# Attention outputs from four 64x64 tiles, a PSUM bank shared with the scores, and outputs placed behind the scores

## The chip, the cores and the metric

The kernel runs on one core of a Trainium2 chip. The metric is device time in microseconds (us). Five engines work side by side: TensorE (PE, matrix products), VectorE (DVE), ScalarE (ACT), GpSimd (POOL) and SyncE (SP, which issues the DMAs). Each takes its own instructions strictly in order. Matrix products land in PSUM, which has eight banks of 128 partitions x 512 float32; a bank is free for the next product when everybody has read the last one out of it.

## The reference

A trunk of two residual layers for 1024 tokens of width 1024: first a retention and RWKV-7 mixer, then sliding-window attention, each followed by a gated feed-forward block, and a last RMSNorm. The change lies in the attention of the second layer:

```python
q, k, v = jnp.split(z, [SWA_WIDTH, SWA_WIDTH + SWA_KV_HEADS * HEAD_DIM], axis=-1)
...
kb, vb = with_prev(k), with_prev(v)
s = jnp.einsum('bnqhgd,bnkhd->bnhgqk', q, kb).astype(jnp.float32) * HEAD_DIM ** -0.5
band = (rel >= 0) & (rel < W)
...
m = jnp.maximum(jnp.max(s, axis=-1, keepdims=True), sink)
e = jnp.exp(s - m)
p = e / (jnp.sum(e, axis=-1, keepdims=True) + jnp.exp(sink - m))
o = jnp.einsum('bnhgqk,bnkhd->bnqhgd', p.astype(vb.dtype), vb)
```

There are 16 query heads of 64, in four groups that share one key and value head each. The queries go in blocks of 128; a query sees the 128 keys that end at its own place, so of a block's 256 keys (its own block and the one before) exactly 128 are used by each query.

## The kernel before, in words

Large products run in a split form: each float32 operand is cut into a high part, rounded to TensorE's single-pass float type, and the rest, and three products (high x high, high x rest, rest x high) are summed in PSUM. A weight of 128 x 1024 comes by DMA (`wload`, L402), ScalarE casts the high part (L432), VectorE or GpSimd subtracts the rest (L433). TensorE is filled with such products (lines 1306, 1308, 1309 in `prod` and 447, 449, 450 in `gemm`), 24 of them for one weight tile and half of the 1024 tokens; they go to the three PSUM buffers `ps_f`. This text calls them filling products.

Attention stands inside such filling. The 16 work items, called pairs here, are (half of the tokens, key head, two query blocks). For a pair j the plan `ATTN_PLAN` has four steps:

- **S**, `scores`: 24 programmed products (20 where the first block has no predecessor), each on a 64x64 tile of TensorE (L1726), to the banks `ps_r`, `ps_c` and twice `ps_m`. Only the band is computed: for each query the score against key x of its own block and of the block before share one place, because only one of the two is inside the window. ScalarE copies one part out (L1737, L1739), VectorE lays the other over it under a mask (L1740), takes the row maximum (L1758) and joins it with the sink (L1759), ScalarE takes eight exponentials, one per head and block (L1763), VectorE adds, inverts and multiplies (L1766 to L1768), and transposes 32x32 blocks (L1773); a DMA writes the result to DRAM (`pd`).
- **D**, `fetch`: four DMAs read it back with the keys on the partitions (`pc`, L1780).
- **M**, `sides`: VectorE multiplies `pc` by a triangle, which gives the part of the own block `pT` (L1787), and VectorE and GpSimd subtract it, one half each, which leaves in `pc` the part of the block before (L1792).
- **O**, `out`: for each of two blocks and two heads of a row, the own block's values times `pT` and the earlier block's values times `pc`, 8 products of 128 keys x 64 (L1805) into one bank `ps_y`. Half of each product's entries are zeros. ScalarE rounds the high part out of PSUM (L1811) and VectorE subtracts for the rest (L1812).

`kv` computes keys and values of a half: the values are transposed with four matmuls per 128 columns into `vt` (L1678), which ScalarE copies (L1679). The letters q, k, r, w, f, p in the plan are steps of the filling: query and key projections, the attention's output projection, the forming of the next block's inputs (`form0`, behind an RMS sum, L479) and the first feed-forward products (`early`, with a copy L1472 out of PSUM between their two halves).

The order on the engines is set by a scheduler, except where `behind` pins one instruction after another, and on TensorE in this stage, where `ATTN_ORDER` fixes the order of all products: each entry is the number of a PSUM tile, in the order in which the tiles first appear, and how many of its products come next.

Of the kernel before, what the change touches and what calls it, by code (L numbers as in the profile page):

```python
# [32 lines left out]
for _n, _w in (  # L33
# [19 lines left out]
def make_consts():  # L53
# [45 lines left out]
    put("amask", np.concatenate([np.where(x[:, None] == x[None, :], own, 0.0), own.T], axis=1))  # L99
# [38 lines left out]
S8 O5 M6 D7 rr S9 O6 M7 D8 S10 O7 M8 D9 wwwwk S11 kwwww rr f rr S12 rr O8 M9 D10 p S13 O9 M10 D11 pp S14 O10 M11 D12 p  # L138
# [116 lines left out]
class Kern:  # L255
    def __init__(self, ctx, tc, A, out):
# [990 lines left out]
    def normed(self, out, hf, k, g, r):  # L1247
        self.nc.vector.scalar_tensor_tensor(
            out=out, in0=self.kt(self.h[hf])(k), scalar=self.col(g, k), in1=r, op0=ALU.mult, op1=ALU.mult
        )  # L1250

    def form0(self, g, r, n8, sp):

        self.X = {nm: [self.hl(n8, k + o) for k in range(4)] for nm, o in (("11", 0), ("21", 4))}
        for nm, o in (("11", 0), ("21", 4)):
            for k in range(4):
                f = self.u0(sp)
                self.normed(f, 0, k + o, g, r)
                self.nc.sync.dma_start(self.bd[k + o], f)
                self.split(f, *self.X[nm][k], False)  # L1260
# [357 lines left out]
    def attn_open(self, ap):  # L1618
        nc = self.nc
        m = self.const(ap, "amask").rearrange("p (m o t) -> p m o t", m=2, o=1)  # L1620
        self.own = m[:, 0].rearrange("p o (x t) -> p o x t", x=2).to_broadcast([P, 2, 2, 64]).bitcast(mybir.dt.uint32)
        self.key = m[:, 1].rearrange("p o (q t) -> p q o t", q=4).to_broadcast([P, 4, 8, 32])
# [9 lines left out]
        self.nu0 = 0  # L1632
        self.akv, self.aq, self.ch = {}, ([], []), {}

    def proj(self, nr, ti, out, **kw):
# [7 lines left out]
        self.nc.vector.tensor_tensor(out=out, in0=ps, in1=nr[1], op=ALU.mult)  # L1643
        self.nc.scalar.activation(out, out, AF.Identity, **kw)

    def kv(self, hf, nr, ap):
# [4 lines left out]
        vt = self.t(ap, [P, 5, 256], "vt", 2)  # L1651
# [40 lines left out]
    def attn(self, ap, outs, fill, plan):  # L1692
# [52 lines left out]
        def scores(j):  # L1745
# [20 lines left out]
            V.tensor_tensor(out=den, in0=den, in1=es, op=ALU.add)  # L1766
# [10 lines left out]
        def fetch(j):  # L1777
            pc = pcs[j] = self.t(ap, [P, 4, 8, 32], "pc", 2)
            for k in range(4):
                nc.sync.dma_start(  # L1780
                    pc[32 * k : 32 * k + 32].rearrange("p q h t -> p q (h t)"), ds[j][:, :, k].rearrange("q t x -> t q x")
                )

        def sides(j):
            pc = pcs[j]
            pT = pTs[j] = self.t(ap, [P, 4, 8, 32], "pT", 2)
            x = V.tensor_tensor(out=pT, in0=pc, in1=self.key, op=ALU.mult)  # L1787
            if j + 2 in sinks:
                self.behind(x, sinks[j + 2])
            for i, e in enumerate((V, G)):  # L1790
                h = slice(4 * i, 4 * i + 4)
                e.tensor_tensor(out=pc[:, :, h], in0=pc[:, :, h], in1=pT[:, :, h], op=ALU.subtract)  # L1792

        def out(j):
# [16 lines left out]
            S.copy(hi, po)  # L1811
# [283 lines left out]
```

## Time and profile before

| | us |
|---|---|
| median of 3 runs | 2266.25 |
| range of the runs | 2265.46 to 2266.54 |
| the profiled execution | 2264.58 |
| its span in the trace | 2261.8 |
| TensorE busy | 2221.5 |
| VectorE busy | 1683.9 |
| ScalarE busy | 1011.3 |
| GpSimd busy | 1009.9 |

The span runs from the first to the last instruction; the profiled execution has 2.8 us around it. The pairs' scores start at 1363.7 us and their last output ends at 1628.1 us; the rest of the program stays as it is.

### The profile page before, as it was taken

Reading aid. Unit: us, or ns where it says so; the run is one execution under the profiler, and the core shown is the slowest. Engines: PE = TensorE matmul, PEld = TensorE weight load, DVE = VectorE, ACT = ScalarE, POOL = GpSimd, SP = SyncE. Lnnn points to the kernel's source line nnn. Section 1 sums busy time; section 2 is a strip of 40 time slices with the busy share of each in tenths; the row PEclk is TensorE's granted clock in tenths of the full one; section 3 lists DMA queues with packets and bytes.
Section 4 is the critical chain, followed back from the end, with each engine's and each line's share of the span. In section 5 each row is a group of like instructions: output and inputs, shape, how many; then the busy total and the mean of one; then the engine's idle time right before and its main releaser. Section 6 shows DMA issues by size and latency. Waiting matters only on the chain.

```text
span 2261.8 us, 36143 instructions
## 1 busy us (share of the span) xinstructions
PE 2221.5 (98%) x13296; PEld 1784.8 (79%) x13296; DVE 1683.9 (74%) x2476; ACT 1011.3 (45%) x1914; POOL 1009.9 (45%) x784
## 2 busy tenths in 40 slices
PE   8999999999999999999999999998999999999998
PEld 6777777777878888888888887776788888888886
DVE  7877965875667358888887877987457788888876
ACT  5454544424455333333433466656444333333335
POOL 3123221202341067777787610104203677777676
PEclk9999999999999999999999999999999999999999
DMA  8565654443446545665676334444546565658663
GB/s 282 188 219 203 201 158 135 141 118 117 148 181 195 205 160 209 214 210 206 242 259 246 131 113 133 162 140 155 176 150 229 176 213 211 208 202 292 225 216 117
DMA packets 181856, 423.22 MB, mean 187 GB/s; under 512 B 44464, under 2 KB 55344, under 8 KB 181680
## 3 DMA queue, kind: packets, MB, share of 16 engines
q1 hardware_dynamic: 178272, 414.37, 53.4%
q10 hardware_dynamic: 2832, 4.45, 0.5%
q8 instruction: 105, 1.72, 0.3%
q0 software_dynamic: 576, 2.10, 0.2%
q14 instruction: 71, 0.58, 0.1%
HBM read 283.87 MB, written 131.60 MB: 184 GB/s over the span
## 4 chain that ended last, share of the span: by engine, by line
PE 77%; DVE 10%; ACT 4%; issue 3%; DMA 3%; POOL 2%; SPq 1%; DVEq 0%; POOLq 0%; ACTq 0%
PE ps_f L291 11%; PE ps_m L1306 8%; PE ps_m L1309 7%; PE ps_m L1308 7%; PE ps_m L291 6%; PE ps_f L1306 5%; PE ps_f L1308 5%; PE ps_f L1309 5%; PE ps_r L1306 2%; PE ps_c L1309 2%; PE ps_c L1306 2%; PE ps_r L1309 2%; PE ps_r L1308 2%; PE ps_c L1308 2%; PE ps_f L449 2%
## 5 line engine op out<-in xcount | busy, mean ns | idle before, releaser
L291 PE MATMUL ps_f<-n,w 128*128 128x512 f32 x1440 | 358.6, 402 | 8.6 <-ACT w L432 5.7
L291 PEld LDWEIGHTS ps_f<-n,w 128*128 128x128 f32 x1440 | 266.5, 189 | 83.4 <-issue 12.6
L433 POOL TENSOR_TENSOR w<-wr,w 128x512 fp32r<-128x512 f32 x63 | 88.3, 1411 | 294.8 <-ACT w L432 293.4
L432 ACT CAST w<-wr 128x512 fp32r<-128x512 f32 x231 | 140.7, 617 | 153.8 <-PE ps_f L450 48.7
L1306 PE MATMUL ps_f<-n,w 128*128 128x512 f32 x415 | 164.6, 397 | 0.5 <-ACT q L1472 0.5
L1309 PE MATMUL ps_f<-n,w 128*128 128x512 f32 x415 | 162.5, 392 | 0.0
L433 DVE TENSOR_TENSOR w<-wr,w 128x512 fp32r<-128x512 f32 x168 | 118.2, 708 | 59.2 <-ACT w L432 58.7
L1308 PE MATMUL ps_f<-n,w 128*128 128x512 f32 x415 | 162.2, 391 | 0.0
L433 POOL TENSOR_TENSOR w<-wq,w 128x512 fp32r<-128x512 f32 x91 | 130.8, 1449 | 31.0 <-ACT w L432 31.0
L1306 PE MATMUL ps_m<-n,w 128*128 128x512 f32 x333 | 130.4, 392 | 0.0
L1308 PE MATMUL ps_m<-n,w 128*128 128x512 f32 x333 | 129.6, 389 | 0.0
L1309 PE MATMUL ps_m<-n,w 128*128 128x512 f32 x333 | 129.5, 389 | 0.0
L1316 DVE TENSOR_TENSOR nq<-ps_m,u 128x512 f32<-128x512 f32 x88 | 58.9, 684 | 93.9 <-PE ps_m L1309 93.8
L464 POOL TENSOR_TENSOR n<-nq,n 128x512 fp32r<-128x512 f32 x60 | 100.1, 1679 | 7.6 <-ACT n L462 7.6
L1501 POOL TENSOR_TENSOR w<-wd,w 128x512 fp32r<-128x512 f32 (+1 forms) x62 | 87.1, 1414 | 33.1 <-ACT w L1500 32.7
L1306 PEld LDWEIGHTS ps_f<-n,w 128*128 128x128 f32 x415 | 77.9, 188 | 21.9 <-issue 3.8
L1306 PE MATMUL ps_m<-cb,w 128*128 128x512 f32 x236 | 91.9, 389 | 0.3 <-DVE nq L1316 0.3
L1308 PE MATMUL ps_m<-cb,w 128*128 128x512 f32 x236 | 91.8, 389 | 0.0
L1309 PE MATMUL ps_m<-cb,w 128*128 128x512 f32 x236 | 91.8, 389 | 0.0
L1309 PEld LDWEIGHTS ps_f<-n,w 128*128 128x128 f32 x415 | 77.9, 188 | 17.1 <-issue 0.7
L1501 POOL TENSOR_TENSOR w<-ws,w 128x512 fp32r<-128x512 f32 (+1 forms) x48 | 71.6, 1497 | 44.4 <-ACT w L1500 40.7
L1308 PEld LDWEIGHTS ps_f<-n,w 128*128 128x128 f32 x415 | 77.9, 188 | 16.6 <-issue 1.0
(539 smaller groups left out, 6347.9 us busy)
## 6 DMA issues: line engine op xcount, KB each, us to landing
hc<-n SPq DMA_DIRECT2D x84, 512.0 KB, 3.2
wsp<-w SPq DMA_DIRECT2D x54, 512.0 KB, 3.3
w<-wsp SPq DMA_DIRECT2D x54, 512.0 KB, 3.4
n<-hc SPq DMA_DIRECT2D x54, 512.0 KB, 6.2
wq<-in_w_gate SPq DMA_DIRECT2D x44, 512.0 KB, 4.5
u<-u SPq DMA_DIRECT2D x76, 256.0 KB, 3.1
ha<-hc SPq DMA_DIRECT2D x34, 512.0 KB, 5.2
hid<-n SPq DMA_DIRECT2D x66, 256.0 KB, 2.0
```

The lines of the kernel that those rows point to most:

```text
L291: i = self.nc.tensor.matmul(out, lhsT, rhs, **kw)
L432: nc.scalar.copy(hi[:, :n], raw[:, c])
L433: self.lo.tensor_tensor(out=lo[:, :n], in0=raw[:, c], in1=hi.bitcast(F32)[:, :n], op=ALU.subtract)
L449: y = nc.tensor.matmul(ps, hi, rl, start=False, stop=False)
L464: e.tensor_tensor(out=lo, in0=src, in1=hi.bitcast(F32), op=ALU.subtract)
L1306: i = mm(ps, hi, xh, start=first and k == 0, stop=False, skip_group_check=True)
L1308: mm(ps, hi, xl, start=False, stop=False, skip_group_check=True)
L1309: mm(ps, lo, xh, start=False, stop=last and k == len(w) - 1, skip_group_check=True)
L1316: self.last_add = V.tensor_tensor(out=o, in0=x, in1=y, op=ALU.add)
L1501: nc.gpsimd.tensor_tensor(out=lo, in0=v, in1=hi.bitcast(F32), op=ALU.subtract)
```

## The change

`out` becomes 20 products of 64 keys x 64 (16 in the first pair of a head), each on one 64x64 tile of TensorE, and leaves out the squares that hold only zeros. Rows 0 to 63 of the tiles work on the first block of the pair and rows 64 to 127 on the second; the first goes to `ps_y`, the second to `ps_c`, the bank that the scores use as well. For that the keys have to lie by halves: the values of the current half and of the other are laid down for both blocks in `vt` (2 x 4 x 256 for each partition where it was 5 x 256), which takes 20 transposing products in the first half of the tokens and 16 in the second where it was 8 and 8, and the value projection is stored with its columns rearranged (`halves`). The probabilities are fetched with the matching rearrangement, in pieces of 128 where it was 256 floats. `sides` now has a triangle only in two of the four squares: `pT` and the subtraction are 512 elements long where the first was 1024, and both run on VectorE. High part and rest of the outputs are taken out in two pieces, one from each bank. In the order, O stands 12 filling products (once 18) behind S in ten of the pairs where it stood right behind it, and new pins (`behind`) set where the output's copies, the subtractions, some copies of the feed-forward's first half (`u0copies`) and one product of `form0` (`formed`) stand.

```diff
-S8 O5 M6 D7 rr S9 O6 M7 D8 S10 O7 M8 D9 wwwwk S11 kwwww rr f rr S12 rr O8 M9 D10 p S13 O9 M10 D11 pp S14 O10 M11 D12 p
+S8 O5 M6 D7 rr S9 O6 M7 D8 O7 wwrr S10 M8 D9 wkw S11 wkwww rr f S12 rr O8 M9 D10 p S13 O9 M10 D11 pp S14 O10 M11 D12 p
...
-17:12 22:24 23,24:8 25,26:12 27:24 28:12 29,30:12 31,32:12 33:6 28:12 34:24 35,36:8 37,38:12 39:8 40:24 41:12 42,43:12
+22,23:12 19:12 24:24 25,26:8 27,28:12 29:24 30:12 31,32:12 33,34:12 30:12 35:2 36:2 35:2 36:2 35:2 36:6 37:24 38,39:8
...
     def kv(self, hf, nr, ap):
-        vt = self.t(ap, [P, 5, 256], "vt", 2)
+        vt = self.t(ap, [P, 2, 4, 256], "vt", 2)
...
         for i, vc in enumerate(vcs):
-            pt = self.pst("m", [P, 4, P])
-            for b in range(4):
-                nc.tensor.transpose(pt[:, b, :], vc[:, P * b : P * b + P], self.cst["ident"])
-            nc.scalar.copy(vt[:, 1:5, P * i : P * i + P], pt)
+            ds = slice(P * i, P * i + P)
+            for prev in range(2):
+                pt = self.pst("m", [P, 2, 2, P])
+                for m in range(2):
+                    for r in range(2):
+                        c = 256 * r + 64 * (2 * m - prev)
+                        if m >= prev:
+                            nc.tensor.transpose(pt[:, m, r], vc[:, c : c + P], ident)
+                            continue
+                        nc.tensor.matmul(pt[64:, m, r], vc[:, c + 64 : c + P], ident, start=True, stop=True, skip_group_check=True)
+                        if not hf:
+                            nc.tensor.transpose(pt[:64, m, r], vc[:, c + 256 : c + 320], ident)
...
         def sides(j):
             pc = pcs[j]
-            pT = pTs[j] = self.t(ap, [P, 4, 8, 32], "pT", 2)
-            x = V.tensor_tensor(out=pT, in0=pc, in1=self.key, op=ALU.mult)
+            pT = pTs[j] = self.t(ap, [P, 2, 2, 4, 32], "pT", 2)
+            d = pc.rearrange("p r (x q) h t -> p (r x) (q h t)", x=2)[:, 0:4:3]
+            o = pT.rearrange("p x q h t -> p x (q h t)")
+            x = V.tensor_tensor(out=o, in0=d, in1=self.key, op=ALU.mult)
             if j + 2 in sinks:
                 self.behind(x, sinks[j + 2])
-            for i, e in enumerate((V, G)):
-                h = slice(4 * i, 4 * i + 4)
-                e.tensor_tensor(out=pc[:, :, h], in0=pc[:, :, h], in1=pT[:, :, h], op=ALU.subtract)
+            subs[j] = x, V.tensor_tensor(out=d, in0=d, in1=o, op=ALU.subtract)
 
         def out(j):
...
-            po = self.pst("y", [P, 2, 2, P])
-            pv = [x[j].rearrange("p q (b i e) t -> p b e i q t", b=2, e=2) for x in (pcs, pTs)]
-            for i in range(2):
-                kbs = (1,) if hf == 0 and b0 + i == 0 else (1, 0)
-                for kb in kbs:
+            po = [self.pst(x, [P, 2, P]) for x in "yc"]
+            c, o = (x[j].rearrange("p r q (i e) t -> p r e i q t", e=2) for x in (pcs, pTs))
+            lo, hi, every = slice(0, 2), slice(2, 4), slice(0, 4)
+            parts = [
+                (0, lambda e: c[:, 0, e, :, hi], hi), (0, lambda e: o[:, 0, e], lo), (1, lambda e: o[:, 1, e], hi),
+                (2, lambda e: c[:, 0, e, :, lo], lo), (3, lambda e: c[:, 1, e], every),
+            ]
+            for y, (kind, src, x) in enumerate(parts):
+                for i in range(2):
+                    first = hf == 0 and b0 + i == 0
+                    if first and kind > 1:
+                        continue
+                    rs = slice(64 * i, 64 * i + 64)
                     for e in range(2):
                         mm(
-                            po[64 * e : 64 * e + 64, i], vt[:, b0 + i + kb, 64 * g : 64 * g + 64], pv[kb][:, i, e],
-                            start=kb == 1, stop=kb == kbs[-1], skip_group_check=True,
+                            po[i][64 * e : 64 * e + 64, :, 32 * x.start : 32 * x.stop],
+                            vt[rs, b0 // 2, kind, 64 * g : 64 * g + 64], src(e)[rs],
+                            start=y == 0, stop=y > 3 or first and y > 0, skip_group_check=True,
                         )
...
-            S.copy(hi, po)
-            V.tensor_tensor(out=lo, in0=po, in1=hi.bitcast(F32), op=ALU.subtract)
+            for i in range(2):
+                his[j] = S.copy(hi[:, i], po[i])
+                los[j] = V.tensor_tensor(out=lo[:, i], in0=po[i], in1=hi[:, i].bitcast(F32), op=ALU.subtract)
...
+        at = -1
+        for w in plan.split():
+            j = int(w[1:]) if w[0] in do else -1
+            if w[0] == "S":
+                at, seen = j, set()
+            elif j >= 0 and at >= 0 and w[0] not in seen:
+                seen.add(w[0])
+                if w[0] == "O":
+                    self.behind(exps[at], his[j])
+                if w[0] == "M":
+                    self.behind(dens[at], subs[j][1])
+            if w[0] == "M" and j and j < 13:
+                self.behind(subs[j][0], los[j - 1])
+        for j, i in ((12, 0), (14, 3), (15, 4)):
+            self.behind(exps[j], self.u0copies[i])
+        self.behind(self.formed[5], los[8])
```

On TensorE, around the output of the second pair, the end of the scores and the output stand like this before (`n` and `w` are inputs of filling products):

```order
L1726 MATMUL ps_m_13255<-ks_1913_12469,q_1969_12808 64x64
L1726 MATMUL ps_m_13254<-kc_1908_12433,q_1969_12808 64x64
L1805 MATMUL ps_y_13292<-pT_13171,vt_12393 64x256 x2
L1805 MATMUL ps_y_13292<-pc_13034,vt_12393 64x256 x2
L1805 MATMUL ps_y_13292<-pT_13171,vt_12393 64x256 x2
L1805 MATMUL ps_y_13292<-pc_13034,vt_12393 64x256 x2
L1306 MATMUL ps_f_13322<-n_1943_12697,w_13316 128x512
```

and with the change the output itself is

```order
L1317 MATMUL ps_f_13362<-n_1946_12714,w_13356 128x512
L1845 MATMUL ps_y_13319<-pc_13049,vt_12393 64x2x64 x2
L1845 MATMUL ps_c_13320<-pc_13049,vt_12393 64x2x64 x2
L1845 MATMUL ps_y_13319<-pT_13199,vt_12393 64x2x64 x2
L1845 MATMUL ps_c_13320<-pT_13199,vt_12393 64x2x64 x2
L1845 MATMUL ps_y_13319<-pT_13199,vt_12393 64x2x64 x2
L1845 MATMUL ps_c_13320<-pT_13199,vt_12393 64x2x64 x2
L1845 MATMUL ps_y_13319<-pc_13049,vt_12393 64x2x64 x2
L1845 MATMUL ps_c_13320<-pc_13049,vt_12393 64x2x64 x2
L1845 MATMUL ps_y_13319<-pc_13049,vt_12393 64x256 x2
L1845 MATMUL ps_c_13320<-pc_13049,vt_12393 64x256 x2
L1314 MATMUL ps_f_13362<-n_1947_12715,wx_13359 128x512
```

The output moved from right behind its scores to 12 filling products behind them, and half of it writes `ps_c`, whose last content is the first part of those scores.

On ScalarE at the same place, before: the copies of the scores, the output's high part, the eight exponentials (`s`, with the sink's `st` among them).

```order
L1739 COPY s_13238<-ps_m_13254 128x2x128
L1644 ACTIVATE kc_2028_13198<-kc_2028_13198,pv_67 128x512
L1811 CAST n_2016_13154<-ps_y_13292 128x2x2x128
L1763 ACTIVATE s_13238,st_13272<-s_13238,st_13272 128x128 x3
L1761 ACTIVATE st_13272<-st_13272 128x8
L1763 ACTIVATE s_13238,st_13272<-s_13238,st_13272 128x128 x5
```

With the change:

```order
L1768 COPY s_13265<-ps_m_13281 128x2x128
L440 CAST w_13638<-wr_13636 128x512
L1792 ACTIVATE s_13265,st_13299<-s_13265,st_13299 128x128 x3
L1790 ACTIVATE st_13299<-st_13299 128x8
L1792 ACTIVATE s_13265,st_13299<-s_13265,st_13299 128x128 x4
L1853 CAST n_2018_13169<-ps_y_13319 128x2x128
L1853 CAST n_2018_13169<-ps_c_13320 128x2x128
L1792 ACTIVATE s_13265,st_13299<-s_13265,st_13299 128x128
```

The output's copies moved from ahead of the exponentials to ahead of the last one.

On VectorE at the same place, before: the masks of the scores, the maximum, the output's rest, and behind the joining with the sink the work of step M.

```order
L1740 COPY_PREDICATED s_13238<-c_amask_12331,ps_m_13254 128x2x128
L1758 TENSOR_REDUCE st_13272<-s_13238 128x8
L1812 TENSOR_TENSOR n_2020_13158<-ps_y_13292,n_2016_13154 128x2x2x128
L1759 TENSOR_TENSOR st_13272<-st_13272,nsink_12335 128x8
L1760 TENSOR_TENSOR st_13272<-st_13272,sink_12333 128x8
L1787 TENSOR_TENSOR pT_13303<-pc_13175,c_amask_12331 128x1024
L1792 TENSOR_TENSOR pc_13175<-pc_13175,pT_13303 128x4x128
```

With the change:

```order
L1787 TENSOR_REDUCE st_13299<-s_13265 128x8
L441 TENSOR_TENSOR w_13638<-wr_13636,w_13638 128x512
L1788 TENSOR_TENSOR st_13299<-st_13299,nsink_12335 128x8
L1789 TENSOR_TENSOR st_13299<-st_13299,sink_12333 128x8
L1854 TENSOR_TENSOR n_2022_13173<-ps_y_13319,n_2018_13169 128x2x128
L1854 TENSOR_TENSOR n_2022_13173<-ps_c_13320,n_2018_13169 128x2x128
L1821 TENSOR_TENSOR pT_13345<-pc_13202,c_amask_12331 128x512
L1656 TENSOR_TENSOR nq_13353<-ps_f_13362,rs_12737 128x4x2x64
L1824 TENSOR_TENSOR pc_13202<-pc_13202,pT_13345 128x2x256
L1796 TENSOR_TENSOR st_13299<-st_13299 128x8
```

The output's rest moved from ahead of the joining (L1759, now L1788) to behind it, and step M stands behind the rest.

## Rows read from the trace of the kernel before

**Rows 1.** Windows: stretch, length, PE, PEld, DVE, ACT, POOL busy (x), clock, DMA share, GB/s.

```profile
1393.20:1461.30 68.10, 67.41 (x561) 51.12 (x560) 64.82 (x108) 43.72 (x158) 9.45 (x8) 1.00 0.51 168
1461.30:1522.60 61.30, 57.94 (x392) 46.24 (x392) 52.42 (x86) 35.48 (x113) 6.52 (x5) 1.00 0.42 142
...
1550.00:1628.10 78.10, 72.91 (x431) 53.80 (x431) 44.01 (x62) 40.46 (x106) 31.17 (x20) 0.93 0.53 170
1628.10:1700.00 71.90, 71.90 (x314) 58.73 (x313) 40.54 (x61) 33.74 (x54) 5.17 (x4) 1.00 0.42 146
```

**Rows 2.** Timeline of TensorE, start and length in us; scores L1726, outputs L1805.

```profile
1404.84 0.27 PE L1726 MATMUL ps_c<-ks,q 64*64 64x64 f32 x1
...
1406.11 0.65 PE L1805 MATMUL ps_y<-pT,vt 128*64 128x256 f32 x4
...
1408.53 0.50 PE L1306 MATMUL ps_f<-n,w 128*128 128x512 f32 x1
...
1461.34 0.37 PE L1726 MATMUL ps_c<-ks,q 64*64 64x192 f32 x1
```

**Rows 3.** The same timeline, the second half of the tokens; L479 is the RMS sum.

```profile
1522.59 1.02 PE L479 MATMUL ps_f<-nq,c_ones 128*128 128x512 f32 x2
...
1582.72 0.65 PE L1805 MATMUL ps_y<-pT,vt 128*64 128x256 f32 x4
...
1584.60 0.50 PE L1306 MATMUL ps_f<-n,wx 128*128 128x512 f32 x1
...
1628.10 0.50 PE L1306 MATMUL ps_f<-n,wx 128*128 128x512 f32 x1
```

**Rows 4.** Timeline of VectorE, one round whole and the ends of six rounds.

```profile
1400.36 0.42 DVE L1740 COPY_PREDICATED s<-c_amask,ps_c 128x256 f32<-128x256 uint32 x1
...
1423.69 0.41 DVE L1740 COPY_PREDICATED s<-c_amask,ps_c 128x256 f32<-128x256 uint32 x1
...
1426.27 0.68 DVE L1812 TENSOR_TENSOR n<-ps_y,n 128x512 fp32r<-128x512 f32 x1
1426.87 0.16 DVE L1759 TENSOR_TENSOR st<-st,nsink 128x8 f32<-128x8 f32 x1
...
1429.01 1.45 DVE L1792 TENSOR_TENSOR pc<-pc,pT 128x512 f32<-128x512 f32 x1
1430.44 0.17 DVE L1766 TENSOR_TENSOR st<-st 128x8 f32<-128x8 f32 x1
...
1435.56 0.44 DVE L1740 COPY_PREDICATED s<-c_amask,ps_c 128x256 f32<-128x256 uint32 x1
...
1470.12 0.43 DVE L1740 COPY_PREDICATED s<-c_amask,ps_c 128x256 f32<-128x256 uint32 x1
```

**Rows 5.** Timeline of ScalarE, the first and the last exponential of that round.

```profile
1427.12 0.40 ACT L1763 ACTIVATE s<-s,st 128x128 f32<-128x128 f32 x1 [4.43 <-DVE st L1759]
...
1429.93 0.39 ACT L1763 ACTIVATE s<-s,st 128x128 f32<-128x128 f32 x1
```

**Rows 6.** Groups by line and shape, 1360 to 1630 us: busy us, mean ns, idle before.

```profile
L1812 DVE TENSOR_TENSOR n<-ps_y,n 128x512 fp32r<-128x512 f32 x16 | 10.9, 681 | 3.2 <-ACT n L1811 3.2
L1740 DVE COPY_PREDICATED s<-c_amask,ps_c 128x256 f32<-128x256 uint32 x16 | 6.9, 432 | 2.4 <-ACT s L1737 2.4
...
L1739 ACT COPY s<-ps_m 128x256 f32<-128x256 f32 x32 | 10.3, 375 | 0.1
L1811 ACT CAST n<-ps_y 128x512 fp32r<-128x512 f32 x16 | 9.5, 592 | 11.5 <-PE ps_y L1805 11.5
...
L1792 POOL TENSOR_TENSOR pc<-pc,pT 128x512 f32<-128x512 f32 x16 | 24.3, 1521 | 136.1 <-DVE pT L1787 56.2 <-DVE st L1766 26.3 <-DMA pc<-pd 26.0
```

**Rows 7.** Waits of TensorE, 1340 to 1680 us: total us, times, longest.

```profile
PE ps_f L1306 <- ACT q L1472: 5.2, 2, 4.6
PE ps_y L1805 <- DVE n L1812: 3.2, 1, 3.2
```

**Rows 8.** The group of the value transposes, 1340 to 1640 us.

```profile
L1678 PE MATMUL ps_m<-c_ident,nq 128*128 128x128 f32 x16 | 2.5, 276 | 1.6 <-DVE s L1740 1.6
```

More of the change, by code (lines that the diff above doesn't have):

```diff
@@ L98, in make_consts @@
     x = np.arange(P) // 64
-    put("amask", np.concatenate([np.where(x[:, None] == x[None, :], own, 0.0), own.T], axis=1))
+    put("amask", np.concatenate([np.where(x[:, None] == x[None, :], own, 0.0), np.repeat(np.tile(own[:64, :64].T, (2, 1)).reshape(P, 2, 1, 32), 4, axis=2).reshape(P, 256)], axis=1))
     put("eps", np.tile(np.array([[RMS_EPS, RET_EPS, RWKV_EPS, math.log(0.5)]], np.float32), (P, 1)))
@@ L278, in __init__ @@
         self.u0s = None
+        self.u0copies, self.formed = [], []
         self.u0d = self.dram("u0", [NP, 2, P, HT])
@@ L1247, in normed @@
     def normed(self, out, hf, k, g, r):
-        self.nc.vector.scalar_tensor_tensor(
+        return self.nc.vector.scalar_tensor_tensor(
             out=out, in0=self.kt(self.h[hf])(k), scalar=self.col(g, k), in1=r, op0=ALU.mult, op1=ALU.mult
@@ L1257, in form0 @@
                 f = self.u0(sp)
-                self.normed(f, 0, k + o, g, r)
+                self.formed.append(self.normed(f, 0, k + o, g, r))
                 self.nc.sync.dma_start(self.bd[k + o], f)
@@ L1471, in early @@
         self.prod(ps, w[0](), self.X["11"], True, False)
-        self.nc.scalar.copy(u0, ps)
+        self.u0copies.append(self.nc.scalar.copy(u0, ps))
         yield
@@ L1619, in attn_open @@
         nc = self.nc
-        m = self.const(ap, "amask").rearrange("p (m o t) -> p m o t", m=2, o=1)
-        self.own = m[:, 0].rearrange("p o (x t) -> p o x t", x=2).to_broadcast([P, 2, 2, 64]).bitcast(mybir.dt.uint32)
-        self.key = m[:, 1].rearrange("p o (q t) -> p q o t", q=4).to_broadcast([P, 4, 8, 32])
+        m = self.const(ap, "amask").rearrange("p (o t) -> p o t", o=1)
+        self.own = m[:, :, :P].rearrange("p o (x t) -> p o x t", x=2).to_broadcast([P, 2, 2, 64]).bitcast(mybir.dt.uint32)
+        self.key = m[:, :, P:].to_broadcast([P, 2, 256])
         self.sink = self.t(ap, [P, 16], "sink")
@@ L1632, in attn_open, with proj @@
         self.nu0 = 0
+        self.u0copies, self.formed = [], []
         self.akv, self.aq, self.ch = {}, ([], []), {}
-    def proj(self, nr, ti, out, **kw):
+    def proj(self, nr, ti, out, halves=False, **kw):
         w = self.wload(self.A["w_qkv"][ti])
@@ L1642, in proj @@
                 yield
-        self.nc.vector.tensor_tensor(out=out, in0=ps, in1=nr[1], op=ALU.mult)
+        o, x, y = out, ps, nr[1]
+        if halves:
+            o = out.rearrange("p (r b t) -> p b r t", r=2, b=4)
+            x, y = (v.rearrange("p (b r t) -> p b r t", b=4, r=2) for v in (x, y))
+        self.nc.vector.tensor_tensor(out=o, in0=x, in1=y, op=ALU.mult)
         self.nc.scalar.activation(out, out, AF.Identity, **kw)
@@ L1671, in kv @@
             vc = self.t(self.pp, [P, HT], "nq", 4)
-            yield from self.proj(nr, 10 + i, vc, bias=self.col("bqkv", 10 + i))
+            yield from self.proj(nr, 10 + i, vc, True, bias=self.col("bqkv", 10 + i))
             vcs.append(vc)
             yield
+        every = slice(0, P), slice(0, 2)
+        ident = self.cst["ident"]
         for i, vc in enumerate(vcs):
-            pt = self.pst("m", [P, 4, P])
-            for b in range(4):
-                nc.tensor.transpose(pt[:, b, :], vc[:, P * b : P * b + P], self.cst["ident"])
-            nc.scalar.copy(vt[:, 1:5, P * i : P * i + P], pt)
+            ds = slice(P * i, P * i + P)
[10 more added lines that the diff above has]
+                            nc.tensor.transpose(pt[:64, m, r], vc[:, c + 256 : c + 320], ident)
+                for rs, m in ((slice(64, P), slice(0, 2)), (slice(0, 64), slice(1, 2))) if prev * hf else (every,):
+                    nc.scalar.copy(vt[rs, m, 2 * prev : 2 * prev + 2, ds], pt[rs, m])
+            if hf and i:
+                G.tensor_copy(vt[:64, 0, 2:4, :], pvt[:64, 0, 2:4, :])
             yield
@@ L1700, in attn @@
         ds, pcs, pTs, n8, sinks = {}, {}, {}, {}, {}
+        exps, dens, his, los, subs = {}, {}, {}, {}, {}
         def block(hf, g, b, tags, s):
@@ L1765, in scores @@
                     self.behind(y, x)
-            V.tensor_tensor(out=den, in0=den, in1=es, op=ALU.add)
+                    exps[j] = y
+            dens[j] = V.tensor_tensor(out=den, in0=den, in1=es, op=ALU.add)
             V.reciprocal(out=den, in_=den)
@@ L1777, in fetch @@
         def fetch(j):
-            pc = pcs[j] = self.t(ap, [P, 4, 8, 32], "pc", 2)
+            pc = pcs[j] = self.t(ap, [P, 2, 4, 4, 32], "pc", 2)
             for k in range(4):
+                b, k2 = k // 2, k % 2
                 nc.sync.dma_start(
-                    pc[32 * k : 32 * k + 32].rearrange("p q h t -> p q (h t)"), ds[j][:, :, k].rearrange("q t x -> t q x")
+                    pc[32 * k : 32 * k + 32].rearrange("p r q h t -> p r q (h t)"),
+                    ds[j][:, :, k2::2, P * b : P * b + P].rearrange("q t r x -> t r q x"),
                 )
```

4 lines of the change are left out of this document (1 added, 3 removed), and 21 rows, old and new, of the table ATTN_ORDER.

## The prediction

> **What bounds the kernel now.** I read the windows first, then TensorE's timeline, VectorE's timeline, the groups and TensorE's waits. In the stretch of the first half's outputs (1393 to 1461 us) TensorE is busy 67.4 of 68.1 us, and VectorE 64.8 of 68.1 [rows 1]: two engines near their limit. Without attention a filling product takes 71.9 / 314 = 0.229 us [rows 1]. The reader is to see in TensorE's timeline that an output stands where its scores end, and that 16 recorded products take 1408.53 - 1406.11 = 2.42 us there [rows 2] where an undisturbed one takes 1584.60 - 1582.72 = 1.88 [rows 3]; the 0.5 is a wait for step M. VectorE goes in rounds, one for each pair, from the mask on `ps_c` to the next one: 1423.69 to 1435.56 is 11.87 us, and the six rounds from 1400.36 to 1470.12 take 69.76, 11.63 each [rows 4]. TensorE stands ahead of VectorE: the scores of pair 9 begin at 1461.34 [rows 2], their mask at 1470.12 [rows 4], 8.8 us later. That lead is what lets TensorE stay busy.
>
> In the second half the loss is in single waits: 5.2 us of filling products for ScalarE's copy L1472 and 3.2 us of an output for VectorE's rest L1812 [rows 7], and the clock, granted 0.93 on average from 1550 to 1628 us [rows 1], which is (1 - 0.93) x 78.1 = 5.5 us at most, part of it lying in the waits. From the RMS sum at 1522.59 to the end of the last output at 1628.10 pass 105.5 us [rows 3].
>
> **The change part by part**, against the profiled execution's 2264.58 us (the median of the runs is 1.67 higher, so that much is added at the end).
>
> *Shorter outputs.* An output streams, on each of the four tiles, four pieces of 128 columns and one of 256, 768 in all; before, 1024 on each of two. No row shows a 64x64 output, but a block of scores has the same tiles and, whole, the same 768 columns: 40 recorded products of the smaller kind take 1406.11 - 1404.84 = 1.27 [rows 2], and 48 on that scale 1.5. So 1.88 becomes 1.5, 12 times: -4.6 us of TensorE's time; the four pairs without a predecessor had 12 records and gain nothing. Bounds: 1.27, and 1.88 if the tiles only overlapped in pairs.
>
> *Value transposes.* 20 more, at 2.5 / 16 = 0.16 us busy each [rows 8], less the tail that each bunch counts twice, 0.13: +2.6, between +2 and +4 (eight of them are true products, twice as long). Twelve lie in front of the first scores, where TensorE never waits: +1.5.
>
> *Step M.* GpSimd loses 24.3 us of subtractions [rows 6], VectorE's multiplication goes from 1024 elements to 512 (some 0.6 less, by the 512-long step that follows) and its subtraction falls from 1.45 [rows 4] to about the 0.6 that a 512-long step takes there (1426.27 to 1426.87 [rows 4]). With the rest in two pieces (+0.1) a round has 1.3 us less VectorE work. The 0.5 us waits of outputs for step M go.
>
> *Evacuation in two pieces.* ScalarE: 2 x 375 for 592 ns, VectorE: 2 x 432 for 681 ns by the half-sized copies and masks [rows 6], so +0.16 and +0.18 us for each pair, +2.5 and +2.9 us over the 16. I take it as hidden behind TensorE, except where a round is bound by VectorE, where the steps overlap and it is the +0.1 above; uncovered it would be +5.4. The Trainium skill ("TensorEngine Tiling (Array Packing)", Performance Considerations, PSUM Bottleneck) says that tiling speeds up TensorE but not the emptying of PSUM, which may become the bound. If that is all that counts here, the 4.6 us are gone and the sum would be 4.6 higher; by the rows above, the copies are only 5 us over 16 pairs on two engines.
>
> *The moved output and its copies.* This is the large term, and it is a loss. Before, VectorE joins maximum and sink at 1426.87 (L1759), the exponentials start at 1427.12, the eighth starts at 1429.93 [rows 5], and the sum L1766 at 1430.44 [rows 4]: 3.57 us, filled by the multiplication, a projection and the subtraction. With the change, ScalarE's order is seven exponentials, the two copies of the output, the last exponential; and VectorE's is maximum, sink, the output's rest, and only then step M. So the rest waits 0.25 + 2.8 (seven of them and the sink's) + 0.4 (a copy) = 3.5 us behind L1759, or 4.1 in every second round, where a projection's bias stands between. Ahead of it in that time stand 0.4 or 1.4 us of VectorE's work; 3.1 and 2.7 us are idle, and step M's 2 us come afterwards. A round is then 11.6 - 1.3 + 2.9 = 13.2 us, less the few tenths that it idled before. Walked through the new order row by row with these steps, the six rounds from pair 3 to pair 9 take 12.05 + 14.19 + 12.05 + 14.19 + 13.20 + 10.75 = 76.4 where they took 69.8: **+6.7 us**. TensorE needs 67.4 / 6 = 11.2 a round [rows 1] and can't run ahead as it did: half of the output goes to `ps_c`, and can't start before that pair's mask on `ps_c` is done; and the next scores can't start before the output's rest has left `ps_c`. The scores of pair 9 can then begin 3.8 us ahead of their mask, not 8.8: **+5.0**. The first mask moves by +0.9 (the transposes +1.5, a shorter step M -0.6). Of the 61.3 - 57.9 = 3.4 us that TensorE idles behind pair 9 [rows 1] some 2 go, 1 us of new waits comes, and two bunches of transposes (+1.1) stand where there was a wait of 1.6 [rows 8]: at the RMS sum +9.8 in all.
>
> *Second half.* From the RMS sum on the change has 280 filling products where there were 300 (20 come earlier), so before is 105.5 - 20 x 0.23 = 100.9 us for equal work. Walking the new order: the output of pair 8 waits 1.5 us for the mask of pair 12 on `ps_c`; the scores of pair 13 wait 2.0 for the rest of that output; the filling behind them 2.0 for a copy L1472 that stands behind seven exponentials; the next output 0.9. Then nothing waits: the pinned copies stand ahead of the exponentials of pairs 14 and 15, so the 4.6 us wait of L1306 [rows 7] goes, the 3.2 us wait goes, and with both the lowered clock. Outputs that were 1.88 are 1.5. Sum: 280 x 0.232 + 4 scores (6.0) + 8 outputs (11.8) + RMS 0.5 + waits 6.4 + 0.5 = 90.2: **-10.7 us**.
>
> *Sum:* +9.8 - 10.7 = -0.9, so 2263.7 for a profiled execution, and with 1.67 about **2265** for a median. Of the gain in the second half nearly all is removed waits, of the loss in the first nearly all is the new round.
>
> **The rivals.**
> *Faster, the round doesn't bind.* If VectorE's order lets it catch up (the last half of the exponentials overlaps more than I take, or TensorE's lead survives), the first half costs only its transposes: outputs -4.6, transposes +2.6, and what is lost now goes, which is idle time of 0.7 + 3.4 + 5.2, some 6 x 0.5 inside outputs and 5.5 by the clock [rows 1], 18 in all, or -20 net: 2246; with half of the new rounds' loss, 2255. For it: VectorE's work falls by 1.3 us a round and GpSimd stops sharing step M. Against it: both orders are fixed, and the rest can't be taken before the copy.
> *Slower, the clock falls in the new gaps.* TensorE is idle 1.8 us a round in pieces of 0.6 to 2.6 us, and 6.4 of 28 us behind the RMS sum. Before, the clock went to half, 1.2 of 2.4 GHz, twice behind waits of 3.2 and 4.6 us [rows 7], and gaps up to 1.6 [rows 8] left it at 1.00 until 1522 [rows 1]. Should it fall in the gaps of 2 us behind the RMS sum and around the first output, as often as in the second half before, 4 to 6 us come back, and with transposes and outputs at their upper bounds (+1.4, +4.6): 2274. [...]
> *The tiles don't overlap four ways.* Then an output lasts 2.6 and not 1.5, 16 us more; the scores' rows speak against it.
>
> **How the numbers follow.** A measurement can tell some 0.2% (4.5 us) from no change. My forecast, gain and loss nearly equal, 2261.7 to 2270.8: 0.42. Faster: 0.33, most of it between 2255 and 2261. Slower: 0.25, of which 0.03 for the tiles. The range 2255 to 2274 leaves out the full gain on one side and the tiles on the other; the forecast's own is 2260 to 2270.
>
> **What would show it.** Right: in VectorE's timeline the rest of an output starts 3.5 to 4.1 us behind the joining L1788, with 2.5 to 3 us of idle put down to ScalarE's L1853; rounds of 12 and 14 us; outputs and scores of TensorE that wait for `ps_c`; an undisturbed output of 1.5 us; no wait over 2.5 us and a clock of 1.00 after 1540 us. Wrong: rounds under 11.7 us, or a clock below 1.00 in the first half.

## The result and the profile after

The changed kernel takes **2274.6 us** (median of 6 runs, 2273.9 to 2276.2) where the kernel before takes 2266.2: a ratio of **1.0038, 95% interval 1.0025 to 1.0051**, slower. The forecast was 2265 in a range of 2255 to 2274. The profiled execution has a span of 2273.2 us, 11.4 more than before; 1.4 of it lie ahead of 1327 us, in code that the change doesn't touch, and are the difference of two executions (1326.14 and 1327.51 us for the same RMS sum), so that some 10 us belong to the change.

The same marks in both traces divide the difference. VectorE's masks on `ps_c` are its marks inside, TensorE's RMS sums those around; what the new order moved ahead of the second RMS sum (20 filling products, 4.6 us) is taken out in the last two rows.

| stretch | forecast, us | measured, us |
|---|---|---|
| RMS sum at 1327 us to the one ahead of the first scores | +1.5 | 36.64 to 40.70: **+4.1** |
| from there to the mask of pair 3 | -0.6 | 37.58 to 37.71: +0.1 |
| six rounds, mask of pair 3 to mask of pair 9 | +6.7 | 69.76 to 76.74: **+7.0** |
| mask of pair 9 to the second RMS sum | +2.2 | 52.47 to 61.18, less 4.6: +4.1 |
| second RMS sum to the last one | -10.7 | 155.15 to 145.17, plus 4.6: **-5.4** |
| sum | -0.9 | +9.9 |

The last row's forecast ends at the last output; from there to the last RMS sum both kernels take 49.6 us.

TensorE's timeline of the kernel before, at the RMS sums (the third of the four is in [rows 3]) and at one bunch of value transposes:

```profile
1326.14 1.02 PE L479 MATMUL ps_y<-nq,c_ones 128*128 128x512 f32 x2
...
1344.90 0.60 PE L1678 MATMUL ps_m<-c_ident,nq 128*128 128x128 f32 x4
1345.25 0.48 PE L1308 MATMUL ps_f<-n,w 128*128 128x512 f32 x1
...
1362.78 1.02 PE L479 MATMUL ps_y<-nq,c_ones 128*128 128x512 f32 x2
...
1677.74 0.59 PE L479 MATMUL ps_y<-nq,c_ones 128*128 128x512 f32 x1
```

The same places of the changed kernel, with both bunches ahead of the first scores:

```profile
1327.51 1.02 PE L487 MATMUL ps_y<-nq,c_ones 128*128 128x512 f32 x2
...
1346.27 0.60 PE L1699 MATMUL ps_m<-c_ident,nq 128*128 128x128 f32 x4
1346.79 0.43 PE L1701 MATMUL ps_m<-c_ident,nq 128*64 128x128 f32 x2
1347.16 0.30 PE L1703 MATMUL ps_m<-c_ident,nq 128*64 128x128 f32 x1
1347.39 0.43 PE L1701 MATMUL ps_m<-c_ident,nq 128*64 128x128 f32 x2
1347.75 0.30 PE L1703 MATMUL ps_m<-c_ident,nq 128*64 128x128 f32 x1
1347.89 0.38 PE L1699 MATMUL ps_m<-c_ident,nq 128*128 128x128 f32 x2
1348.03 0.47 PE L1316 MATMUL ps_f<-n,w 128*128 128x512 f32 x1
...
1350.25 0.66 PE L1699 MATMUL ps_m<-c_ident,nq 128*128 128x128 f32 x4 [1.06 <-ACT vt L1705]
...
1368.21 1.02 PE L487 MATMUL ps_y<-nq,c_ones 128*128 128x512 f32 x2
...
1543.84 0.59 PE L487 MATMUL ps_f<-nq,c_ones 128*128 128x512 f32 x1
...
1689.01 0.59 PE L487 MATMUL ps_y<-nq,c_ones 128*128 128x512 f32 x1
```

L1699 and L1703 are transpositions, recorded once each; L1701 is an ordinary product, recorded twice. A bunch went from 0.35 us (start of the first to start of the next filling product) to 1.76, and the second one waits 1.06 for ScalarE's copy: 2 x 1.4 + 1.1 = 3.9 us of the 4.1.

VectorE's timeline of the changed kernel, the round that answers to the whole round in [rows 4]:

```profile
1405.92 0.43 DVE L1769 COPY_PREDICATED s<-c_amask,ps_c 128x256 f32<-128x256 uint32 x1
...
1418.73 0.45 DVE L1769 COPY_PREDICATED s<-c_amask,ps_c 128x256 f32<-128x256 uint32 x1
...
1423.06 0.16 DVE L1788 TENSOR_TENSOR st<-st,nsink 128x8 f32<-128x8 f32 x1
1423.25 0.17 DVE L1789 TENSOR_TENSOR st<-st,sink 128x8 f32<-128x8 f32 x1
1426.51 0.43 DVE L1854 TENSOR_TENSOR n<-ps_y,n 128x256 fp32r<-128x256 f32 x1 [3.08 <-ACT n L1853]
...
1427.18 0.68 DVE L1821 TENSOR_TENSOR pT<-pc,c_amask 128x512 f32<-128x512 f32 x1
...
1428.98 0.16 DVE L1796 TENSOR_TENSOR st<-st 128x8 f32<-128x8 f32 x1
...
1432.79 0.41 DVE L1769 COPY_PREDICATED s<-c_amask,ps_c 128x256 f32<-128x256 uint32 x1
...
1482.66 0.45 DVE L1769 COPY_PREDICATED s<-c_amask,ps_c 128x256 f32<-128x256 uint32 x1
```

The same round on ScalarE, which answers to [rows 5]:

```profile
1423.31 0.40 ACT L1792 ACTIVATE s<-s,st 128x128 f32<-128x128 f32 x1 [1.66 <-DVE st L1788]
...
1426.12 0.35 ACT L1853 CAST n<-ps_y 128x256 fp32r<-128x256 f32 x1
...
1426.64 0.41 ACT L1792 ACTIVATE s<-s,st 128x128 f32<-128x128 f32 x1
```

The rest starts 3.45 us behind L1788, with 3.08 us idle ahead of it. Step M stands behind it, and the sum L1796 comes 2.5 us behind the rest. The round is 14.06 us; the six are 12.81, 14.06, 12.01, 14.06, 13.18 and 10.62.

Where TensorE waits, 1340 to 1690 us (us in total, times, longest), against [rows 7]:

```profile
PE ps_c L1845 <- DVE s L1769: 7.8, 7, 2.8
PE ps_c L1755 <- DVE n L1854: 5.7, 4, 2.1
PE ps_f L1314 <- ACT q L1480: 1.5, 2, 1.1
PE ps_m L1699 <- ACT vt L1705: 1.1, 1, 1.1
```

13.5 us of the 16 are new waits for the bank `ps_c`: 7.8 for the mask of the scores and 5.7 for the rest of an output. On TensorE's timeline, the start of pair 9's scores, and one output that nothing holds up, with the filling product behind it:

```profile
1478.99 0.37 PE L1755 MATMUL ps_c<-ks,q 64*64 64x192 f32 x1 [2.00 <-DVE n L1854]
...
1597.90 0.33 PE L1845 MATMUL ps_y<-pc,vt 64*64 64x128 f32 x2
...
1599.41 0.50 PE L1314 MATMUL ps_f<-n,w 128*128 128x512 f32 x1
```

And the windows of the changed kernel (columns as in [rows 1]):

```profile
1398.70:1479.00 80.30, 72.19 (x695) 55.21 (x694) 61.58 (x120) 48.83 (x183) 1.05 (x2) 0.96 0.46 148
...
1405.00:1415.00 10.00, 8.59 (x45) 6.53 (x46) 6.63 (x15) 5.27 (x22) 0.53 (x1) 0.66 0.63 210
1564.00:1567.00 3.00, 2.84 (x48) 2.65 (x48) 2.16 (x5) 3.00 (x15) 0.00 (x0) 0.50 0.83 279
1586.00:1590.00 4.00, 3.79 (x46) 3.01 (x47) 2.71 (x7) 1.30 (x8) 0.17 (x1) 1.00 0.95 357
```

In the stretch of the first half's outputs TensorE idles 8.1 us where it idled 0.7, and the clock, 1.00 there before, is 0.66 over the 10 us from 1405 us, at the end of the first output's wait of 2.8 us. From 1564 to 1567 us, behind a wait of 2.1 us, it is at its lower level again (0.50), and pair 13's scores take 2.8 us for the 1.5 of the others.

### The profile page after: what moved, and what is told of

It is laid out like the page before. It is cut to its first block, busy times and chain, and to the rows that moved or that the text cites. A ratio compares the mean times of both kernels' runs of the same rounds, so it can differ in the third digit from the quotient of the medians.

```text
span 2273.2 us, 36895 instructions
## 1 busy us (share of the span) xinstructions
PE 2229.9 (98%) x13692; PEld 1794.1 (79%) x13692; DVE 1673.3 (74%) x2492; ACT 1016.5 (45%) x1936; POOL 982.8 (43%) x768
## 4 chain that ended last, share of the span: by engine, by line
PE 78%; DVE 10%; ACT 4%; DMA 3%; issue 3%; POOL 1%; SPq 1%; DVEq 0%; ACTq 0%; POOLq 0%
PE ps_f L299 11%; PE ps_m L1314 8%; PE ps_m L1317 7%; PE ps_m L1316 7%; PE ps_m L299 6%; PE ps_f L1314 5%; PE ps_f L1317 5%; PE ps_f L1316 5%; PE ps_r L1314 2%; PE ps_r L1317 2%; PE ps_c L1317 2%; PE ps_c L1314 2%; PE ps_r L1316 2%; PE ps_c L1316 2%; PE ps_f L455 2%
## 5 line engine op out<-in xcount | busy, mean ns | idle before, releaser
L299 PEld LDWEIGHTS ps_f<-n,w 128*128 128x128 f32 x1440 | 268.5, 190 | 83.4 <-issue 12.7
```

The costliest lines, as they stand in the source:

```text
L299: i = self.nc.tensor.matmul(out, lhsT, rhs, **kw)
```

## The experiments

All change the order or the layout only. Each group of runs was compared with the kernel before on the same chip (medians 2265.4, 2265.7 and 2266.2 us); "rounds" are the six between the masks of pairs 3 and 9.

**1. The output's copies ahead of all exponentials.** The pin of the change names `exps[at]`, and that is the exponential of head 0 alone; the order on ScalarE shows seven of the eight ahead of the copies.

```diff
+                alls.setdefault(j, []).append(y)
...
-                    self.behind(exps[at], his[j])
+                    for y in alls[at]:
+                        self.behind(y, his[j])
```

> The changed kernel, with the output's two copies pinned ahead of all eight exponentials, not of one. Theory A (the rest waits behind seven exponentials, and step M behind the rest, which makes the rounds 12.8 us on average): the rest starts within 1.2 us of the joining L1788, step M fills VectorE's wait for the exponentials, the six rounds between the masks of pairs 3 and 9 fall from 76.7 us to 67 to 70, and the median from 2274.6 to 2264 to 2268. Theory B (TensorE's waits for the shared bank set the round): the rounds stay over 74 us and the median over 2272. Theory C (the exponentials now wait for the moved output): rounds longer than now, over 2278.

Measured: **2261.55 us**, ratio to the kernel before 0.9983 (0.9974 to 0.9992), by the two ratios some 12.5 us below the change. TensorE's waits for `ps_c` fall from 13.5 to 5.0 us. VectorE's timeline, the same round:

```profile
1418.06 0.45 DVE L1769 COPY_PREDICATED s<-c_amask,ps_c 128x256 f32<-128x256 uint32 x1
...
1422.64 0.42 DVE L1855 TENSOR_TENSOR n<-ps_y,n 128x256 fp32r<-128x256 f32 x1 [0.54 <-ACT n L1854]
...
1426.01 0.17 DVE L1797 TENSOR_TENSOR st<-st 128x8 f32<-128x8 f32 x1 [0.19 <-ACT s L1792]
...
1429.93 0.44 DVE L1769 COPY_PREDICATED s<-c_amask,ps_c 128x256 f32<-128x256 uint32 x1
```

The rest starts with 0.5 us of idle ahead of it, step M lies inside the exponentials, the sum waits 0.2 us. This round is 11.87 us for 14.06, the six 69.99 for 76.74. It moves the median past the range expected (2264 to 2268), because the second half shortens too, from 145.2 to 142.0 us. Theories B and C fall.

**2. Step M freed of the rest.** The other way to fill the idle time: the lines that pin `subs[j][0]` (the first instruction of step M) behind `los[j - 1]` (the rest of the output before) are left out.

> The changed kernel without the pin that puts step M behind the rest of the output before it. Theory A: step M goes into VectorE's idle 2.6 to 3.1 us ahead of the rest, the sum of the exponentials follows the rest at once, the six rounds fall from 76.7 us to 68 to 71, median 2265 to 2269. Theory B (the shared bank's waits set the round): no change, 2272 to 2276.

Measured: **2271.05 us** (ratio 1.0025, 1.0016 to 1.0034). The rounds fell as theory A had it, to 70.01 us, though TensorE still waits 9.4 us for `ps_c`, so theory B falls. The median lies above theory A's range: from the second RMS sum on it takes 148.0 us, 2.8 more than the change, and this line is back among VectorE's waits there (1545 to 1597 us):

```profile
DVE pT L1821 <- DMA pc<-pd: 5.6, 2, 4.1
```

So this pin costs the rounds of the first half and pays in the second: with it VectorE has no wait for a fetch in that window. That led to runs 3 to 5.

**3 and 4. The pins of the second half, put on the kernel before.** Run 3 adds the four pins of the change's last lines; run 4 puts the copies of pairs 14 and 15 ahead of all eight exponentials.

```diff
+        for j, i in ((12, 0), (14, 3), (15, 4)):
+            self.behind(exps[j], self.u0copies[i])
+        self.behind(self.formed[5], los[8])
```

> The kernel before, with only the pins of the second half added (the copies out of the feed-forward's first half ahead of one exponential of pairs 12, 14 and 15, one product of form0 behind the rest of pair 8's output). Theory A (these pins alone take away the waits of 4.6 and 3.2 us and the lowered clock): 2256 to 2260. Theory D (a pin on one exponential of eight moves a copy by only 0.4 us, so only the 3.2 us wait shrinks): 2262 to 2266.

> As the run before it, with the copies of pairs 14 and 15 ahead of all eight exponentials. Theory D: the copy leaves at about 1571 us, not 1575, the 4.6 us wait and the lowered clock behind it go, the median is 2256 to 2261, below both kernels. If the wait were for something else than the copy: 2262 to 2267.

Measured: 2268.2 us (1.0012, 1.0002 to 1.0021) and 2266.3 us (1.0007, 0.9998 to 1.0016): no gain. Run 3 lies above both of its ranges; run 4 lies in the range for a wait that is for something else than the copy. In both, TensorE's 3.2 us wait for the rest shrank to 0.9, and one of 2.1 or 2.2 came for the inputs that the pin on `form0` delays (L465). The copy of run 4 did leave earlier, at 1572.0 us for 1575.1, and the scores of pair 15 began at 1575.6 for 1581.1; but TensorE's waits for copies became longer in sum, 5.2 to 7.5 us:

```profile
PE ps_f L1307 <- ACT q L1473: 7.5, 2, 4.9
PE ps_f L1309 <- DVE n L465: 2.1, 1, 2.1
```

(the same view of run 4). TensorE then waited as long, 4.9 us, for another copy of the same kind: it stands at pair 15's exponentials, and these waited for VectorE's joining, at 1588.05 us in run 4 and 1585.55 before.

**5. The kernel before, step M one pair later in the second half.** VectorE's waits of the kernel before, 1545 to 1597 us:

```profile
DVE pT L1787 <- DMA pc<-pd: 15.4, 3, 6.1
DVE st L1766 <- ACT s L1763: 3.7, 1, 3.7
```

In the rounds of pairs 13 to 15 its step M stands ahead of the sum of the exponentials and waits for a fetch. SyncE's queue there, at the first of the three (pair 12's result goes out, and behind it the fetch that step M reads):

```profile
1554.78 0.32 SPq L1775 DMA_DIRECT2D pd<-sq  x1
1555.67 2.13 SPq L1780 DMA_DIRECT2D pc<-pd  x4
```

Step M starts at 1561.82 us, when that has landed, and the sum, the transposition and the next mask come behind it. VectorE's step M and joining, ScalarE's copy behind the exponentials and the filling product that waits for the copy, from the timelines of the kernel before:

```profile
1561.82 1.22 DVE L1787 TENSOR_TENSOR pT<-pc,c_amask 128x1024 f32<-128x1024 f32 x1 [3.62 <-DMA pc<-pd]
...
1570.37 0.17 DVE L1759 TENSOR_TENSOR st<-st,nsink 128x8 f32<-128x8 f32 x1
...
1575.10 0.56 ACT L1472 COPY q<-ps_f 128x512 f32<-128x512 f32 x1
...
1575.71 0.79 PE L1306 MATMUL ps_f<-n,wx 128*128 128x512 f32 x1 [4.61 <-ACT q L1472]
```

```diff
+        for j in (10, 11, 12):
+            self.behind(tops[j], sinks[j + 3])
+        self.behind(tops[13], last[15])
```

> The kernel before, with step M of pairs 10 to 12 pinned one pair later (behind the maximum of the pair three on, as the changed kernel has it) and of pair 13 behind the last transposition. Theory E (in the second half VectorE waits 22 us for the fetch of step M, with the sum of the next pair's exponentials behind it, and TensorE's waits of 4.6 and 3.2 us and the lowered clock only follow from that): VectorE's waits for the fetch between 1545 and 1595 us fall from some 21 to under 5 us, the rounds from 15 to 11 to 12.5 us, TensorE's waits in the second half go, the median is 2256 to 2260. Theory F (the copies on ScalarE or the load of its tables bind there): no change, 2263 to 2267.

Measured: **2256.9 us**, ratio 0.9968 (0.9955 to 0.9980). The waits in the same window (where the expectation's 21 us are 15.4 before):

```profile
DVE st L1767 <- ACT s L1764: 8.6, 4, 3.7
DVE pT L1788 <- DMA pc<-pd: 3.2, 1, 3.2
```

The rounds between the masks of pairs 12 and 15 are 12.7, 13.6 and 12.4 us, where they were 16.2, 13.0 and 15.2. From RMS sum to RMS sum it is 149.5 us for 155.2. Theory E holds for the 4.6 us wait, of which 0.5 is left: this wait for a copy on ScalarE, which the prediction read as its own cause, was the end of a chain that began at a DMA. It doesn't hold for the rest: the 3.2 us wait for the rest of pair 8 stayed (3.3), and so did a lowered clock, 0.94 from 1540 to 1600 us (0.91 before).

**6. With copies first, the first output 12 filling products later.** In the order `30:12 35:2 ... 36:6 37:24` becomes `30:12 37:12 35:2 ... 36:6 37:12`.

> The changed kernel with the output's copies ahead of all exponentials, and besides the first output behind 24 filling products instead of 12. Theory: in the run without the second edit TensorE waits 2.9 us at that output for the mask on the shared bank and then runs some 5 us at half its clock, which later rounds don't recover: both go, the scores of pair 4 begin 4 to 5.5 us earlier, median 2256 to 2259 where it was 2261.5. Rival (VectorE's rounds bind behind it, and TensorE only waits elsewhere): 2260.5 to 2262.5.

Measured: 2259.25 us (0.9972, 0.9962 to 0.9983). The clock from 1398 to 1415 us is 1.00, and the scores of pair 4 follow those of pair 3 by 13.5 us instead of 18.1, as expected; of these 4.6 us, 1.5 reach the mask of pair 9, and 2.3 the median (the intervals of this ratio and run 1's overlap). Both are a part right: the wait and its clock go, but most of the 4.6 us is lost again by pair 9.

**7. The change without the pins of the second half.**

> The changed kernel without the pins of the second half (copies ahead of an exponential of pairs 12, 14 and 15, a product of form0 behind the rest of pair 8). Theory (the second half gained by step M's place and length, not by these pins): 2272 to 2277, and no wait over 3 us for the copies. Rival (these pins had taken away the wait of 4.6 us): it is back, 2278 to 2283.

Measured: 2276.4 us (1.0048, 1.0035 to 1.0060), no wait of TensorE for a copy L1480 from 1545 to 1640 us. These pins are worth some 2 us (1.8 by the medians; 147.5 for 145.2 us from the second RMS sum to the last one), and the intervals of the two ratios overlap. The wait of 4.6 us is gone without them.

**8. The ten moved outputs back behind their scores.**

> The changed kernel with the ten moved outputs back right behind their scores. Theory A (the place of the copies behind the exponentials is the loss, the move only gives TensorE work while the mask on the shared bank is done): each of these outputs waits 1 to 1.5 us more for the mask, rounds are shorter where the copies happen to fall ahead of the exponentials, 2268 to 2275. Rival (the move of the output is itself the loss): 2262 to 2267.

Measured: **2287.2 us** (1.0093, 1.0079 to 1.0107), worse than either expected. TensorE's waits for the mask, 7.8 us in the change:

```profile
PE ps_c L1831 <- DVE s L1755: 23.1, 10, 6.0
```

The first output waits 6.0 us, the clock is 0.55 from 1404 to 1414 us, at the end of that wait, and the rounds are 80.9 us. With a bank that the scores share, the move is worth some 12.5 us; it isn't the loss.

**9. Values by DMA.** On run 6: the blocks that serve as the earlier block are the same values 64 partitions away, and are copied there by DMAs, instead of being transposed again.

```diff
-            for prev in range(2):
...
+            if i:
+                nc.sync.dma_start(vt[64:, :, 2:4], vt[:64, :, 0:2])
+                nc.sync.dma_start(vt[:64, 1, 2:4], vt[64:, 0, 0:2])
+                if hf:
+                    nc.sync.dma_start(vt[:64, 0, 2:4], pvt[64:, 1, 0:2])
```

> The run with the copies first and the first output later, and besides the second half of the value layout (the blocks that serve as the earlier block) copied by two or three DMAs out of the first, in place of 12 and 8 transposing products. Theory (the transposes cost TensorE 4.0 us ahead of the first scores, 1.1 of it a wait for a copy, where the prediction had 1.5): from the RMS sum at 1327 us to the one ahead of the scores 36.5 to 38 us instead of 40.7, and some 1 us less in the second bunches; median 2254 to 2257 where it was 2259.3. Rival (the first VectorE rounds bind there, so that TensorE only waits later): 2258 to 2260.

Measured: **2254.1 us**, ratio 0.9949 (0.9936 to 0.9961), the fastest of all, and faster than both kernels. From the RMS sum at 1324.8 us to this one pass 36.6 us:

```profile
1361.39 1.02 PE L473 MATMUL ps_y<-nq,c_ones 128*128 128x512 f32 x2
```

The whole 4.1 us of the transposes come back, and from the mask of pair 9 to the second RMS sum another 2.0.

**10. Run 5, with pair 8's output copied out early.**

> The kernel before, with step M of pairs 10 to 13 later, and besides pair 8's output copied out ahead of pair 12's exponentials and its rest ahead of the joining with the sink. Theory (the 3.3 us wait of pair 9's output for that rest is the last wait over 2 us, and the clock falls behind it): the wait is under 0.5 us, the clock from 1540 to 1600 us is 1.00 where it was 0.94, median 2250 to 2254 where it was 2256.9. Rival (TensorE then waits for the copies of the feed-forward's first half instead): 2255 to 2258.

Measured: 2258.2 us (0.9966, 0.9952 to 0.9979), the same as run 5 and just above the rival's range, with the rival's mechanism: the clock from 1540 to 1600 us is 0.94 as in run 5, the 3.3 us wait went, and in its place stands

```profile
PE ps_f L1306 <- ACT q L1472: 4.8, 3, 3.4
```

## Why the prediction was wrong

**The new round: right.** The rest behind the joining by 3.45 us, 3.1 us of it idle and put down to L1853, step M behind it, rounds of 12 and 14 us: each as forecast, and the six rounds take 76.7 us where 76.4 were walked. Of the six only the first is off, 12.81 for 12.05. The lead of pair 9's scores over their mask is 1482.66 - 1478.99 = 3.7 us for a forecast 3.8. Runs 1 and 2 show the cause: either edit that takes step M (with the projection between its two halves 1.8 us, 1427.18 to 1428.98) out of the chain brings the six rounds back to 70.0. The prediction had the order, seven exponentials ahead of the copies; run 1 shows that it is the loss.

**Shorter outputs: right where nothing holds them up.** Such an output takes 1599.41 - 1597.90 = 1.51 us in the trace of the changed kernel, 1.5 forecast. The rival that the tiles overlap only in pairs falls.

**Value transposes: mis-sized**, "+1.5" ahead of the first scores where 4.1 came. The step took 0.16 us for each added product from a group's mean of busy time, and that "TensorE never waits" there. In the rows the six added products make a bunch 1.4 us longer, some 0.24 each. Besides, a bunch now fills both buffers of `ps_m` where it filled one, so the second bunch waits 1.1 us for the first one's copy. Run 9 has the whole term.

**Second half: the step that failed.** -10.7 us were forecast, -5.4 measured: the outputs gave 2.8 (16.2 to 13.4), TensorE's waits 1.6 (8.4 to 6.8). The sum that gave 90.2 us is 95.5 in the trace, from the RMS sum to the end of the last output (1543.84 to 1639.39):

| term | forecast, us | measured, us |
|---|---|---|
| 280 filling products | 65.0 | 67.5 |
| 4 scores | 6.0 | 7.3 |
| 8 outputs | 11.8 | 13.4 |
| RMS sum 0.5, and an unnamed 0.5 | 1.0 | 0.5 |
| waits | 6.4 | 6.8 |

The filling was taken at 0.232 us a product, which no row shows; it took 0.241. It now stands in 13 pieces where it stood in 10, and the first and last product of a piece take some 0.1 us more (0.34 at 1548.60 and 0.32 at 1546.78, for 0.23 in the middle). The scores have 1.3 us of the lowered clock, which was to go. Four of the outputs take 1.7 to 2.0 us, their waits left out; in these the products on `ps_c` start later than those on `ps_y`.

The waits are right in sum by luck. "The pinned copies stand ahead of the exponentials of pairs 14 and 15, so the 4.6 us wait goes [...] Then nothing waits": ahead of the scores of pair 14, where 6.4 us were walked, waits of 2.1, 0.4 and 0.3 us came; from these scores on, where none was forecast, TensorE waits 0.8 (these scores, for the rest), 2.2 (an output, for the mask) and 1.1 us (a copy). The 4.6 us wait did go, but not by these pins: they hold one exponential of eight, so a copy moves by 0.4 us, and run 7, without them, has no such wait. On the kernel before, step M's later place takes it away, 5.7 us by itself (run 5); that it does so in the change as well is argued from run 7 and from run 2, where with step M free the waits for the fetch are back. In the trace of before, VectorE's wait for the fetch, 15.4 us in three, was the row to look up behind [rows 7]; the prediction followed the wait one engine back only.

**Between pair 9 and the RMS sum**: +4.1 for +2.2. The lead fell by 5.1 us, as forecast. Behind it 2.8 us were to come back and 1.0 did: TensorE's waits fell by 3.2 us, but the two bunches of transposes take 2.6 us for 0.8 before, where +1.1 was forecast; run 9 gets 2.0 us back. The terms printed for "+9.8 in all" add up to 11.1 at the least, so that 1.3 us of it have no stated source.

**The rivals.** The slower rival, the clock falling in the new gaps, came true in its mechanism, at the two places it named (around the first output, and behind the RMS sum), behind waits of 2.8 and 2.1 us, and so did the prediction's own sign of being wrong, a clock below 1.00 in the first half. Its 2274 is where the time came out, though not by that alone: run 6, without the first of the falls and its wait, gains 2.3 us on run 1. The faster rival, that VectorE catches up, is false for the change; run 1 makes its first half true, with rounds of 11.7 us. The Trainium skill's rule that with tiling the emptying of PSUM may become the bound ("TensorEngine Tiling (Array Packing)", Performance Considerations, PSUM Bottleneck) agrees with the trace only in this sense: 13.5 of the 16 us that TensorE waits are for `ps_c` to be emptied. But it is the place of the copies and not their length: run 1, with the same copies in another place, leaves 5.0.

**Still open**: with the copies first, TensorE's waits around pairs 12 and 13 (some 5 us in run 9) and those of run 10. No run takes the lowered clock away by itself, without the wait ahead of it.

## What to carry to other kernels

A pin that names one instruction of a loop orders one instruction: print the order of that engine and see that the others moved with it. When a wait is to be removed, follow it back until the releaser isn't itself waiting; a wait of 4.6 us for a copy here led back from the copy over exponentials, joining and step M to a fetch, and with the copy alone moved TensorE waited 4.9 us for the next one. An output that shares a bank with the scores should stand far enough behind them that their mask is done, and its copies out ahead of whatever long work the same engine has next.

## What was not expected of the hardware

The value products in their new shapes cost more of TensorE's time than the whole ones: an ordinary product on half of the array's columns (L1701, 128x64, recorded as two) moves the next one back by 0.37 us, a transposition on half of them (L1703) by 0.23 or 0.14, where four whole transpositions take 0.52 in the same bunch and 0.35 in the kernel before, in front of a filling product. How much of that is the shape itself and how much the change from one shape to another, no run separates.

The first output's wait of 2.8 us cost nearly as much again by the clock: the 24 filling products behind it take 8.1 us, the 24 behind the next output 5.8. The length of a wait didn't tell whether the clock fell: behind one of 2.1 us it was 0.50 (1564 to 1567 us), behind one of 2.2 us 1.00 (1586 to 1590 us), and behind one of 2.0 us pair 9's scores took the 1.5 us of the others.
